# First weight pair of a macaron feed-forward: seven Strassen products for gate and up alike, with two products of the next pair's gate taken ahead

## The chip, the cores and the metric

The kernel runs on one core of a Trainium2 chip. Time is device time in microseconds (us) for one execution. The engines are TensorE (PE, with its weight load PEld), VectorE (DVE), ScalarE (ACT), GpSimd (POOL) and SyncE (SP), which issues nearly all DMAs.

## The reference

One layer: half a SwiGLU feed-forward, two attention mixers side by side, a projection, and a second half feed-forward, each behind an RMS norm, for 1024 tokens of width 1024 in float32. The change touches the first part of the two feed-forwards (D_FF = 2816):

```python
def rms_norm(x, g):
    xf = x.astype(jnp.float32)
    y = xf * lax.rsqrt(jnp.mean(xf * xf, axis=-1, keepdims=True) + EPS)
    return (y * g.astype(jnp.float32)).astype(x.dtype)

def swiglu(h, w_gate, w_up, w_down):
    return (jax.nn.silu(h @ w_gate) * (h @ w_up)) @ w_down

x = x + 0.5 * swiglu(rms_norm(x, g_ffn1[l]), w1_gate[l], w1_up[l], w1_down[l])
...
x = x + 0.5 * swiglu(rms_norm(x, g_ffn2[l]), w2_gate[l], w2_up[l], w2_down[l])
```

## The kernel before, in words

**Numbers as two halves.** TensorE is fed float32 numbers as a rounded high half and a low half that holds the rest. An operand tile has the high half in its columns 0 to 511 (`HI`) and the low half in 512 to 1023 (`LO`). ScalarE writes the high half and GpSimd or VectorE subtracts it to get the low one (`halve`, L379). A product of two operands is then high x high, high x low and low x high over four blocks of 128: 12 matmuls (`times`, L526).

**Strassen's scheme (Winograd's form).** `ffn_in` (L501) makes gate and up, turned so that features lie on partitions. It takes weights in pairs of 128 features: a pair's left matrix has the blocks A11, A12 (first 128 features, first and second half of the width) and A21, A22 (the second 128). The right matrix is the normed input, turned: B11, B21 for the first 512 tokens, B12, B22 for the second 512. With S1 = A21 + A22, S2 = S1 - A11, S3 = A11 - A21, S4 = A12 - S2 and T1 = B12 - B11, T2 = B22 - T1, T3 = B22 - B12, T4 = B21 - T2, the table `FACTORS` (L375) names seven products instead of eight. Product 1 is A11 B11, 2 is A12 B21, 3 is S4 B22, 4 is A22 T4, 5 is S1 T1, 6 is S2 T2 and 7 is S3 T3. B12 itself is in none of them. C11 is 1 + 2 in one PSUM bank; the others are sums of u2 = 1 + 6 with the rest, in which 4 adds into the bank of 7 and 3 into the bank of 5.

**The pairs.** There are 11 pairs in each feed-forward. Pairs 2 to 11 go through `products` (L538), in the order 1, 6, 7, 5, 2, 4, 3, once for gate and once for up. The first pair goes through `opening` (L562), because the second token half comes late: in the first feed-forward its rows are still being loaded and normed, in the second they come out of the projection before it.

**The opening before.** Gate is computed by eight plain half products (`half`, L574) with B11, B21, B12 and B22, up by seven. Six products need the first token half alone: gate's four and up's 1 and 2. Then both turns of the second half (`R.turn`, L435: 16 transposes each) follow, and then nine products. The opening stands under `tc.manual_schedule`: each engine takes its operations in the order of the program text. Outside it a scheduler places the operations, and it can put those of the second pair between the opening's, as their operands allow.

**Around it.** `R.stat` (L420) sums the squares of a token tile on ScalarE, with a small step on VectorE and a power on GpSimd; `R.norm` (L426) scales the tile on VectorE. In the first feed-forward this runs for tiles 4 to 7 within the opening, in the second for tile 7 (the list `rows`). `R.keep` copies turned blocks out of PSUM for the sums T1 to T4, and `R.low` (L483) makes operands of those sums. PSUM has eight banks, two for each letter "a" to "d" (`bank`, L331). `finish` (L675) makes the seven left operands of the down projection for a pair and stores them. `beside` (L879) hangs other work of the kernel onto the pairs' products by count, from the second pair on. The loads of weight tiles (512 KB each) have four places; the second pair's loads reuse those of the first as soon as its blocks are halved.

Of the kernel before, what the change touches and what calls it, by code (L numbers as in the profile page):

```python
# [58 lines left out]
def f32(ap):  # L59
    return ap.bitcast(F32)  # L60
# [187 lines left out]
def trunk(ctx, tc, x, positions, g_ffn1, w1_gate, w1_up, w1_down, g_mix, w_in, g_cq, w_uq_a, w_q_idx,  # L248
# [136 lines left out]
    class Right:  # L385
# [87 lines left out]

        def kept(self):
# [17 lines left out]
    def loader(raw, nm):  # L492
        def load(w, f, name):
            t = raw(name)
# [6 lines left out]
    def ffn_in(nm, R, wg, wu, raw, op, sums, ct, bank, staged, rows, first=None, beside=lambda n, ins: None):  # L501
# [5 lines left out]
        def left_sides(rs, name, pinned, early=False):  # L507
            A11, A12, A21, A22 = (r[:, q] for r in rs for q in (HI, LO))
            O = {n: op(f"{name}{n}") for n in ("A11", "S2", "S3", "S1", "A12", "A22", "S4")}
            s1, s2, s3, s4 = (sums(f"{name}s{n}") for n in range(1, 5))  # L510
            in_turn_ = tc.keep_in_program_order if pinned else lambda i: i
            if early:
                halve(O["A11"], A11)

            def rest():
# [4 lines left out]
                for n, src in (("A11", A11), ("S2", s2), ("S3", s3), ("S1", s1), ("A12", A12), ("A22", A22), ("S4", s4))[early:]:  # L520
                    halve(O[n], src)
                return O

            return rest if early else rest()
# [13 lines left out]
        def products(O, name, nxt):  # L538
            pa = bank("pa", "a")
            mul(O, 1, pa)  # L540
            u2 = ct(f"{name}u2")
            nc.scalar.activation(u2, pa, AF.Copy)
# [11 lines left out]
            mul(O, 2, pa, False)  # L554
# [5 lines left out]
            return (pa, u2, c21, u3), nxt  # L560

        def opening(raws, rows, nxt):  # L562


            A = [dict(zip(("A11", "A12", "A21", "A22"), (r[:, q] for r in rs for q in (HI, LO)))) for rs in raws]
            O = ({}, {})

            def left(e, *names):
                for n in names:
                    O[e][n] = halve(op(f"{nm}{e}0{n}"), A[e][n])  # L570

            ps, sg = {}, {}

            def half(r, c, q, letter=None):  # L574

                if not q:
                    ps[r, c] = bank("pg", letter)
                times(O[0][f"A{r + 1}{q + 1}"], B[f"B{q + 1}{c + 1}"], ps[r, c], not q)

            def gate(r, c):  # L580
                sg[r, c] = ct(f"{nm}sg")
                nc.scalar.activation(sg[r, c], ps[r, c], AF.Silu)

            def up(n, ps_, start=True):
                a, b = FACTORS[n]
                times(O[1][a], B[b], ps_, start)
# [1818 lines left out]
```

## Time and profile before

| | |
|---|---|
| median of 3 runs | 2128.14 us (2124.06 to 2130.36) |
| the profiled execution | 2127.6 us |
| its span, first to last instruction | 2125.8 us |
| mean granted clock of TensorE | 0.998 |
| TensorE, VectorE, ScalarE, GpSimd busy | 99%, 71%, 50%, 43% of the span |
| products of the first opening | 15.2 to 63.4 us |
| products of the second opening | 1485.4 to 1533.5 us |

In a row of a timeline stand the start and the duration in us, the engine, the line of the kernel, the operation, the tile written and the tiles read, the shape, and how many were merged. In brackets is the idle time of the engine before it and what ended that. A name such as `a01A` is tile A of the first feed-forward (a), gate (0), second pair (1). A row of windows gives for each stretch the busy time of PE, PEld, DVE, ACT and POOL, then the granted clock as a share of full speed, the share of the DMA engines and the GB/s.

### The profile page before, as it was taken

Reading aid. Unit: us, or ns where it says so; the run is one execution under the profiler, and the core shown is the slowest. Engines: PE = TensorE matmul, PEld = TensorE weight load, DVE = VectorE, ACT = ScalarE, POOL = GpSimd, SP = SyncE. Lnnn points to the kernel's source line nnn. Section 1 sums busy time; section 2 is a strip of 40 time slices with the busy share of each in tenths; the row PEclk is TensorE's granted clock in tenths of the full one; section 3 lists DMA queues with packets and bytes.
Section 4 is the critical chain, followed back from the end, with each engine's and each line's share of the span. In section 5 each row is a group of like instructions: output and inputs, shape, how many; then the busy total and the mean of one; then the engine's idle time right before and its main releaser. Section 6 shows DMA issues by size and latency. Waiting matters only on the chain.

```text
span 2125.8 us, 29838 instructions
## 1 busy us (share of the span) xinstructions
PE 2105.6 (99%) x10196; PEld 1766.6 (83%) x10196; DVE 1519.8 (71%) x2485; ACT 1056.7 (50%) x1990; POOL 910.6 (43%) x718
## 2 busy tenths in 40 slices
PE   9999999999999999999999999999999999999999
PEld 7888888888889989888878888888888888888887
DVE  7866767678875599788886768844755556487675
ACT  6343343334455356888887667435432322324443
POOL 6654555522346234422113333354664545542233
PEclk9999999999999999999999999999999999999999
DMA  5577877497685252676747744774143333359655
GB/s 150 160 247 216 254 201 239 152 335 248 206 230 167 79 160 92 223 219 178 181 133 232 253 140 134 253 277 139 50 129 99 104 94 126 97 188 327 221 175 188
DMA packets 298104, 387.79 MB, mean 182 GB/s; under 512 B 40144, under 2 KB 186224, under 8 KB 297952
## 3 DMA queue, kind: packets, MB, share of 16 engines
q1 hardware_dynamic: 285088, 343.90, 52.1%
q0 software_dynamic: 12864, 41.99, 5.5%
q8 instruction: 80, 1.31, 0.3%
q14 instruction: 72, 0.59, 0.1%
HBM read 264.67 MB, written 121.15 MB: 181 GB/s over the span
## 4 chain that ended last, share of the span: by engine, by line
PE 90%; DVE 3%; DMA 3%; issue 2%; ACT 1%; POOL 0%; SPq 0%; DVEq 0%; ACTq 0%; POOLq 0%
PE p L769 6%; PE p L770 6%; PE p L768 6%; PE psf L312 4%; PE psf L313 4%; PE psf L314 4%; PE pd L530 4%; PE pd L531 3%; PE pd L529 3%; PE pa L530 3%; PE pc L529 3%; PE pa L531 3%; PE pa L529 3%; PE pc L530 3%; PE pc L531 3%
## 5 line engine op out<-in xcount | busy, mean ns | idle before, releaser
L1369 ACT ACTIVATE junka<-u,cand,sig 128x896 bf16<-128x896 f32 (+3 forms) x124 | 134.6, 1085 | 5.9 <-DVE cand L1361 4.6
L1816 DVE TENSOR_TENSOR_SCAN left<-left,hidden 128x640 f32<-128x640 f32 (+3 forms) x64 | 89.1, 1414 | 2.7 <-ACT left L1810 2.5
L892 ACT ACTIVATE swh<-swr 128x512 fp32r<-128x512 f32 x48 | 30.2, 630 | 116.9 <-issue 48.2
L893 DVE TENSOR_TENSOR swr<-swr,swh 128x512 f32<-128x512 f32 x48 | 44.8, 932 | 39.4 <-ACT swh L892 36.5
L1871 DVE SCALAR_TENSOR_TENSOR pt<-pstT,pt 128x512 fp32r<-128x512 f32 (+1 forms) x96 | 51.7, 550 | 16.5 <-ACT pt L1868 15.7
L672 ACT ACTIVATE b0u<-b0u 128x512 f32<-128x512 f32 x20 | 12.6, 632 | 99.8 <-DVE b0u L552 84.4
L1868 ACT ACTIVATE pt<-pstT 128x512 fp32r<-128x512 f32 (+1 forms) x96 | 46.6, 495 | 24.1 <-PE pstT L1943 23.0
L1721 ACT ACTIVATE relu<-psdot 128x512 f32<-128x512 f32 (+1 forms) x80 | 39.8, 522 | 27.7 <-DVE u L1728 17.9
L769 PE MATMUL p<-aT,aS 128*128 128x512 f32 x132 | 51.6, 391 | 0.9 <-DVE aT L382 0.9
L769 PE MATMUL p<-bT,bS 128*128 128x512 f32 x132 | 51.4, 390 | 0.0
L1230 POOL DMA_DIRECT2D gd<-evg x32 | 18.1, 566 | 76.9 <-ACT evg L1225 66.4
L770 PE MATMUL p<-aT,aS 128*128 128x512 f32 x132 | 50.8, 390 | 0.0
L770 PE MATMUL p<-bT,bS 128*128 128x512 f32 x132 | 50.8, 390 | 0.0
L1728 DVE SCALAR_TENSOR_TENSOR u<-relu,WI,u 128x512 f32<-128x512 f32 (+1 forms) x70 | 46.0, 680 | 2.8 <-ACT relu L1721 1.8
L1943 PE MATMUL pstT<-ident,left 128*128 128x128 f32 x288 | 46.0, 273 | 1.2 <-DVE pt L1871 1.2
L768 PE MATMUL p<-bT,bS 128*128 128x512 f32 x132 | 47.0, 389 | 0.0
L1997 ACT ACTIVATE e<-e,mx 128x1024 f32<-128x1024 f32 (+7 forms) x52 | 40.2, 774 | 10.2 <-DVE mx L1988 9.3
L768 PE MATMUL p<-aT,aS 128*128 128x512 f32 x132 | 44.9, 390 | 0.0
L1943 PEld LDWEIGHTS pstT<-ident,left 128*128 128x128 f32 x288 | 35.6, 140 | 10.6 <-DVE pt L1871 2.4
L1810 ACT ACTIVATE left<-psz 128x512 f32<-128x512 f32 (+2 forms) x96 | 42.9, 506 | 1.9 <-PE psz L1836 1.5
L381 ACT ACTIVATE bT<-bt 128x512 fp32r<-128x512 f32 x44 | 26.3, 625 | 33.9 <-PE p L770 29.4
L1365 DVE TENSOR_SCALAR_CACHE_REDUCE junkv<-u,cand 128x512 uint8<-128x512 f32 (+1 forms) x62 | 41.7, 673 | 0.7
(3065 smaller groups left out, 8141.0 us busy)
## 6 DMA issues: line engine op xcount, KB each, us to landing
aw<-in_w_down_dram SPq DMA_DIRECT2D x33, 512.0 KB, 4.8
bw<-in_w_down_dram SPq DMA_DIRECT2D x33, 512.0 KB, 4.8
swr<-in_w_in_dram SPq DMA_DIRECT2D x48, 256.0 KB, 6.3
a0r<-in_w_gate_dram SPq DMA_DIRECT2D x22, 512.0 KB, 7.8
a1r<-in_w_up_dram SPq DMA_DIRECT2D x22, 512.0 KB, 7.4
b0r<-in_w_gate_dram SPq DMA_DIRECT2D x22, 512.0 KB, 4.2
b1r<-in_w_up_dram SPq DMA_DIRECT2D x22, 512.0 KB, 3.9
x<-in_x_dram SPq DMA_DIRECT2D x16, 512.0 KB, 6.1
```

Of the source, the lines that this page charges most:

```text
L312: nc.tensor.matmul(ps, ah, bh, start=first, stop=False)
L313: nc.tensor.matmul(ps, ah, bl, start=False, stop=False)
L314: nc.tensor.matmul(ps, al, bh, start=False, stop=last)
L529: nc.tensor.matmul(ps, a[:, c], b[k][:, HI], start=start and k == 0, stop=False, skip_group_check=True)
L530: nc.tensor.matmul(ps, a[:, c], b[k][:, LO], start=False, stop=False, skip_group_check=True)
L531: ins = nc.tensor.matmul(ps, a[:, l], b[k][:, HI], start=False, stop=k == 3, skip_group_check=True)
L768: nc.tensor.matmul(ps[q][m], S[:, h], T[:, HI], start=p == 0, stop=False)
L769: nc.tensor.matmul(ps[q][m], S[:, h], T[:, LO], start=False, stop=False)
L770: nc.tensor.matmul(ps[q][m], S[:, l], T[:, HI], start=False, stop=p == last)
L1369: nc.scalar.activation(junks[1][:, 0:(i + 1) * P], score[i], AF.Sign, scale=sig[:, b:b + 1], bias=cand.bitcast(F32)[:, b:b + 1], accum_out ...
L1816: nc.vector.tensor_tensor_scan(back, back, ones, 1.0, op0=ALU.mult, op1=ALU.max)
L1943: nc.tensor.transpose(tp[:, q * P:(q + 1) * P], A[n + q][:, j * P:(j + 1) * P], ident)
```

## The change

In the opening gate goes through the seven products as up does. A third left matrix, the second pair's gate, is halved in part (A11 and A12, loaded once more and earlier into a place of its own), and its products 1 and 2 stand in the opening too. So six products still need the first token half alone, of three matrices, but the third matrix's product 2 comes between the two turns. `products` then leaves out 1 and 2 for that gate. B12 is turned, but no longer made into an operand; three of its four places hold the sums for T2 and the third matrix's load. Gate's S1, S2 and S4 and up's S4 are summed on VectorE, S3 of both on GpSimd. The steps that multiply gate by up and `finish` of the first pair move under the manual order, at its end. The tiles of the token rows are allocated ahead, and SyncE issues the third matrix's load between the loads of token tiles 5 and 6.

```diff
         def turn(self, n, letters="abcd", less=None, between=0, also=None):
-            if n not in self.B:
+            if n not in self.B and n != "B12":
                 self.operands(n)
...
-                t = self.B[n][k]
-                self.keep([(t[:, HI], ps)])
-                self.less([t[:, LO]], [ps], [f32(t[:, HI])])
+                if n in self.B:
+                    t = self.B[n][k]
+                    self.keep([(t[:, HI], ps)])
+                    self.less([t[:, LO]], [ps], [f32(t[:, HI])])
...
+        def third(self, load, w):
+            load(w, 2, f"{self.nm}0r1", self.held[2])
+
+        def hold(self):
+            self.held = [f32(self.tt(f"{self.nm}hold{k}")) for k in range(3)] + [self.tt(f"{self.nm}hold3")]
...
-        def products(O, name, nxt):
-            pa = bank("pa", "a")
-            mul(O, 1, pa)
-            u2 = ct(f"{name}u2")
-            nc.scalar.activation(u2, pa, AF.Copy)
+        def products(O, name, nxt, begun=None):
+            if begun:
+                u2, c11 = begun
+            else:
+                c11 = pa = bank("pa", "a")
+                mul(O, 1, pa)
+                u2 = ct(f"{name}u2")
+                nc.scalar.activation(u2, pa, AF.Copy)
...
-            mul(O, 2, pa, False)
+            if not begun:
+                mul(O, 2, pa, False)
...
+            left("A12", 0, 1)
+            r = R.raw
+            r["T2"] = [t[:, c] for t in R.held[0:2] for c in (HI, LO)]
+
+            def step(t):
                 R.keep(copies[1 + 2 * t:3 + 2 * t], nc.vector)
                 if 4 - t <= len(rows):
                     R.stat(rows[t + len(rows) - 4])
+            step(0)
+            by(0, 1, "a", "a")
+            u2[0] = copied(ct(f"{nm}u2"), 0, "a")
+            step(1)
+            by(1, 1, "a", "b")
+            u2[1] = copied(ct(f"{nm}u2"), 1, "a")
+            left("A11", 2)
+            left("A12", 2)
+            step(2)
+            by(0, 2, "a", start=False)
+            out[0, 0] = copied(ct(f"{nm}sg"), 0, "a", AF.Silu)
+            step(3)
+            fsum("S1", nc.vector, 0, 1)
+            fsum("S2", nc.vector, 0)
+            left("S1", 0, 1)
             for t in rows:
                 R.norm(t)
+            by(1, 2, "a", start=False)
+            fsum("S2", nc.vector, 1)
+            fsum("S4", nc.vector, 0)
+            by(2, 1, "a", "c")
+            u2[2] = copied(ct(f"{nm}u2"), 2, "a")
+            left("S4", 0)
+            nc.vector.tensor_mul(out[0, 0], out[0, 0], ps[1, "a"])
+            fsum("S4", nc.vector, 1)
+            left("S4", 1)
+            R.turn("B12", "dabc", (r["T1"], r["T3"]))
+            by(2, 2, "a", start=False)
             R.low("T1", nc.gpsimd)
+            out[2, 0] = copied(ct(f"{nm}sg"), 2, "a", AF.Silu)
+            R.less(r["T2"], R.turn("B22", "dada"), r["T1"])
+            by(0, 5, "d", "b")
+            by(1, 5, "d", "c")
+            left("S2", 0, 1)
+            u3[0] = copied(R.spare(f"{nm}u3"), 0, "d")
             R.low("T2", nc.vector)
+            u3[1] = copied(R.spare(f"{nm}u3"), 1, "d")
+            fsum("S3", nc.gpsimd, 0, 1)
+            left("S3", 0, 1)
+            by(0, 3, "d", start=False)
+            by(1, 3, "d", start=False)
             R.less(r["T3"], r["T2"], r["T3"])
+            R.less(r["T4"], r["T4"], r["T2"])
             R.low("T3", nc.vector)
+            by(0, 6, "b", "b")
+            nc.vector.tensor_add(u2[0], u2[0], ps[0, "b"])
+            left("A22", 0, 1)
+            by(1, 6, "b", "c")
+            R.low("T4", nc.vector)
+            nc.vector.tensor_add(u2[1], u2[1], ps[1, "b"])
+            nxt = nxt({n: O[2][n] for n in ("A11", "A12")})
+            c12 = [ct(f"{nm}c12") for e in range(2)]
+            for e in range(2):
+                nc.vector.tensor_add(c12[e], u2[e], ps[e, "d"])
+            nc.scalar.activation(c12[0], c12[0], AF.Silu)
+            for e in range(2):
+                by(e, 7, "c", "da"[e])
+                nc.vector.tensor_add(u3[e], u3[e], u2[e])
+                nc.vector.tensor_add(u3[e], u3[e], ps[e, "c"])
+                if not e:
+                    nc.scalar.activation(u3[0], u3[0], AF.Silu)
+            nc.vector.tensor_mul(c12[0], c12[0], c12[1])
             nxt = nxt()
+            nc.vector.tensor_mul(u3[0], u3[0], u3[1])
+            for e in range(2):
+                by(e, 4, "c", start=False)
+                nc.vector.tensor_add(u2[e], u2[e], ps[e, "c"])
+                if not e:
+                    nc.scalar.activation(u2[0], u2[0], AF.Silu)
...
-                    H, u, nxt = opening(first, rows, lambda: lefts(1, 0, early=True))
+                    H, S, begun, nxt = opening(first, R.held[2], rows, lambda made: lefts(1, 0, made=made))
+                    finish(0, H, S, True)
+                continue
...
             for t in range(4, NT):
+                if t == 6:
+                    R.third(load, w1_gate)
                 rows(t)
```

Here `by(e, n, p)` is product n of matrix e (0 gate, 1 up, 2 the second pair's gate) into bank p, with a letter where the bank is new; `left(n, ...)` is `halve` of block n; `fsum` forms one of S1 to S4; `copied` is ScalarE's copy out of a bank, with Silu where named.

More of the change, by code (lines that the diff above doesn't have):

```diff
@@ L559, in products @@
             nc.vector.tensor_add(u2, u2, pd)
[L560 to L569, printed above, removed]
-                    O[e][n] = halve(op(f"{nm}{e}0{n}"), A[e][n])
[L572 to L584, printed above, removed]
+            return (c11, u2, c21, u3), nxt
@@ new lines, in opening, with left, fsum, by @@
+        def opening(raws, third, rows, nxt):
+            A = [dict(zip(("A11", "A12", "A21", "A22"), (r[:, q] for r in rs for q in (HI, LO)))) for rs in (*raws, (third,))]
+            O, S, ps, u2, u3, out = ({}, {}, {}), ({}, {}), {}, {}, {}, {}
+            def left(n, *es):
+                for e in es:
+                    O[e][n] = halve(op(f"{nm}{e}0{n}"), A[e][n])
+            def fsum(n, eng, *es):
+                for e in es:
+                    a, b = {"S1": ("A21", "A22"), "S2": ("S1", "A11"), "S3": ("A11", "A21"), "S4": ("A12", "S2")}[n]
+                    A[e][n] = sums(f"{nm}{e}{n}")
+                    (eng.tensor_add if n == "S1" else eng.tensor_sub)(A[e][n], A[e][a], A[e][b])
+            def by(e, n, p, letter=None, start=True):
+                if letter:
+                    ps[e, p] = bank(f"p{p}", letter)
@@ L585, in up, with copied @@
                 a, b = FACTORS[n]
-                times(O[1][a], B[b], ps_, start)
+                times(O[e][a], B[b], ps[e, p], start)
+            def copied(to, e, p, func=AF.Copy):
+                nc.scalar.activation(to, ps[e, p], func)
+                return to
             if "B11" not in B:
-                left(0, "A11")
-                R.operands("B12", "B11", "B21", "B22", "T1")
+                left("A11", 0)
+                R.operands("B11", "B21", "B22", "T1")
                 R.kept()
@@ L596, in opening @@
                 copies += zip(R.raw["T4"], p21)
-                left(0, "A21", "A22")
                 R.second()
@@ L606, in opening @@
                     R.stat(rows[t + len(rows) - 4])
-                left(1, *n)
-            r = R.raw
-            r["T2"] = [R.spare(f"{nm}r22{k}") for k in range(4)]
-            S = {n: sums(f"{nm}s{n}") for n in ("S1", "S2", "S3", "S4")}
-            A11, A12, A21, A22 = (A[1][n] for n in ("A11", "A12", "A21", "A22"))
-            nc.vector.tensor_add(S["S1"], A21, A22)
-            nc.vector.tensor_sub(S["S2"], S["S1"], A11)
-            A[1].update(S)
+            step(0)
+            by(0, 1, "a", "a")
@@ L618, in opening @@
-            half(0, 0, 1)
-            gate(0, 0)
-            left(1, "S2")
-            half(1, 0, 0, "b")
-            pa = bank("pa", "a")
-            up(1, pa)
-            u2 = ct(f"{nm}u2")
-            half(1, 0, 1)
-            nc.scalar.activation(u2, pa, AF.Copy)
-            gate(1, 0)
-            left(1, "S1")
-            up(2, pa, False)
-            R.turn("B12", "cdab", (r["T1"], r["T3"]))
-            nc.gpsimd.tensor_sub(S["S3"], A11, A21)
-            nc.gpsimd.tensor_sub(S["S4"], A12, S["S2"])
@@ L633, in opening @@
-            left(1, "S3")
-            R.less(r["T2"], R.turn("B22", "bcdc"), r["T1"])
-            R.low("T1", nc.gpsimd)
-            half(0, 1, 0, "d")
-            half(1, 1, 0, "b")
-            R.low("T2", nc.vector)
-            left(1, "S4", "A22")
-            half(0, 1, 1)
-            gate(0, 1)
-            half(1, 1, 1)
-            gate(1, 1)
+            by(1, 2, "a", start=False)
+            fsum("S2", nc.vector, 1)
+            fsum("S4", nc.vector, 0)
+            by(2, 1, "a", "c")
@@ L2332, in trunk @@
             x1 = residual(1)
-            R = Right(g_ffn2, bank, fp(op), ct, ct, tt, ts, in_turn((sums, 3), (ct, 1)), "b")
+            R = Right(g_ffn2, bank, fp(op), ct, ct, tt, ts, ct, "b")
             def between():
-                R.operands("B12")
+                R.hold()
                 R.kept()
```

87 lines of the change are left out of this document (36 added, 51 removed).

## The prediction

> **What bounds the kernel now.** I read the first page, then the timelines of the engines over the first feed-forward's opening (0 to 80 us), then over the second's (1480 to 1560).
>
> ```profile
> span 2125.8 us, 29838 instructions
> PE 2105.6 (99%) x10196; PEld 1766.6 (83%) x10196; DVE 1519.8 (71%) x2485; ACT 1056.7 (50%) x1990; POOL 910.6 (43%) x718
> ```
>
> TensorE (PE) is busy for 2105.6 of 2125.8 us. A matmul left out is therefore time saved, as long as the operands of the next one are ready. TensorE's rows (start, duration, idle time before it and what ended that):
>
> ```profile
> 15.20 0.47 PE L529 MATMUL pg<-aB,a00A 128*128 128x512 f32 x1
> 23.47 0.39 PE L529 MATMUL pa<-aB,a10A 128*128 128x512 f32 x1
> 26.19 0.39 PE L529 MATMUL pg<-aB,a00A 128*128 128x512 f32 x1
> 31.64 3.65 PE L443 MATMUL pst<-ident,x 128*128 128x128 f32 x32
> 35.87 0.47 PE L529 MATMUL pg<-aB,a00A 128*128 128x512 f32 x1 [0.57 <-ACT aB L464]
> 53.89 0.39 PE L529 MATMUL pa<-aB,a01A 128*128 128x512 f32 x1
> 57.29 0.39 PE L530 MATMUL pa<-aB,a01A 128*128 128x512 f32 x1
> 60.46 0.46 PE L529 MATMUL pc<-aT,a10A 128*128 128x512 f32 x1
> 75.44 0.51 PE L529 MATMUL pc<-aT,a01A 128*128 128x512 f32 x1 [0.44 <-DVE a0u L549]
> 1501.67 3.65 PE L443 MATMUL pst<-ident,x 128*128 128x128 f32 x32
> 1505.90 0.47 PE L529 MATMUL pg<-bB,b00A 128*128 128x512 f32 x1 [0.57 <-ACT bB L464]
> ```
>
> A product of 12 matmuls takes 2.72 us (23.47 to 26.19, 0.227 each). Six products run from 15.20 to 31.64, then the 32 transposes of the second token half (0.114 each, 1.82 for a turn of 16), then the rest. TensorE waits 0.57 in each opening and 0.44 in the pair after the first. The rows 53.89 and 57.29 are the second pair's product 1, put among the opening's last products. The opening's last product starts at 60.46, right behind the VectorE (DVE) addition that empties its bank:
>
> ```profile
> 59.63 0.67 DVE L659 TENSOR_TENSOR au<-au,pc 128x512 f32<-128x512 f32 x1
> ```
>
> Without those 12 matmuls it would have been due 2.7 us earlier. So VectorE already ends the opening one product late, and the second pair's product 1 is what covers that.
>
> **The change part by part.** *Saved.* Each opening and its next gate go from 22 to 21 products: 2.72 us, twice is 5.44. If the quoted waits go too (0.57 + 0.57 + 0.44 = 1.58) it is 7.0. The eight operations that made B12 an operand go as well, beside TensorE.
>
> *A bank wait, first opening only.* Up's product 1 moves from fourth place to second and takes the older "b" bank. That bank is free after the first of the two copies in the second row:
>
> ```profile
> 14.60 4.68 DVE L470 SCALAR_TENSOR_TENSOR aB<-pst,agcol,aB 128x512 fp32r<-128x512 f32 x7
> 19.20 1.39 DVE L462 TENSOR_SCALAR araw<-pst,agcol 128x512 f32<-128x512 f32 x2
> ```
>
> The copy ends at 19.9, and VectorE runs it behind the seven operations above. TensorE is there at 15.20 + 2.72 = 17.9: **2.0 us**, and the product ends at 22.6.
>
> *The norm of the last token tile.* ScalarE (ACT) keeps the written order. New in it: the last tile's sum of squares stands behind a copy of product (up, 1), two halvings of the third matrix and the first Silu with its table load.
>
> ```profile
> 17.52 1.20 ACT L381 ACTIVATE a00A<-a0r 128x512 fp32r<-128x512 f32 x2
> 18.56 1.10 ACT L423 ACTIVATE aj<-x 128x1024 bf16<-128x1024 f32 x1
> 19.60 0.68 ACT L381 ACTIVATE a10A<-a1r 128x512 fp32r<-128x512 f32 x1
> 23.93 1.28 ACT L582 ACT_TABLE_LOAD   x1
> 25.22 0.60 ACT L582 ACTIVATE asg<-pg 128x512 f32<-128x512 f32 x1
> ```
>
> From start to start a 512-wide operation takes 0.52 and a sum of squares 1.04. So: copy from 22.9, halvings to 24.4, tile 6's sum to 25.5, table to 26.8, Silu to 27.3, tile 7's sum, readable at 28.5. VectorE, held by its small step on that sum, then has three operand sums (0.60 each) and four norms:
>
> ```profile
> L429 DVE TENSOR_SCALAR x<-x,rs x4: 740/748/1777, 25.6 to 28.6; 128x1024 f32<-128x1024 f32 x4
> 43.54 2.48 DVE L490 TENSOR_TENSOR aT<-ar,aT 128x512 fp32r<-128x512 f32 x4
> 38.12 5.05 POOL L490 TENSOR_TENSOR aT<-araw,aT 128x512 fp32r<-128x512 f32 x4 [1.55 <-ACT aT L488]
> ```
>
> 28.5 + 1.8 + 4 x 0.75 = 33.3. TensorE has three more products before B12's turn, 22.6 + 8.2 = 30.8, and 0.3 of transposes that need no tile 7: **2.2 us** (4.2 if GpSimd slows two norms to 1.78). In the second opening that sum also moves behind the Silu, but the norm (1498.2, below) comes before TensorE (1498.95).
>
> *The low halves of T1.* Product 5 now follows B22's turn at once and needs T1, whose low halves GpSimd (POOL) makes behind those of S1 and S4 for two matrices: eight in a row, 1.26 each, 10.1. If VectorE's stream lets it in only after the norms and two sums (34.5), with about 0.5 more between, they end at 45.1. TensorE: B12 turned at 34.8, product (third, 2), B22's turn, and 2.27 until the fourth low half is used: 41.6. A wait of 3.5. Second opening: it begins at 1501.67 - 6 x 2.72 = 1485.35; the third product ends at 1493.5, ScalarE gives the sum by 1495.6, VectorE the norm by 1498.2 and two sums by 1499.4, GpSimd ends at 1510.0, TensorE needs it at 1507.6: 2.4. If GpSimd gets in at 1497 it is 1.3.
>
> *VectorE's list up to product 4.* Gate's product 4 adds into the bank that gate's u3 must first have read. From the end of B22's turn VectorE has 8 operations on B22 and T2 (0.66: 5.3), 20 of 0.60 for the low halves of T2, T3, T4 and the sums T3, T4 (12.0), and six additions (3.6): 20.9. Then 1.0, because T2's high halves stand on ScalarE behind a copy of product (gate, 5). TensorE has 8 products, 21.8. On VectorE's time alone it would nearly fit. But GpSimd now has work in that stretch without a break: S3's sums and low halves and A22's, six operations where there were two.
>
> ```profile
> 44.88 7.10 POOL L382 TENSOR_TENSOR a10S<-asS,a10S 128x512 fp32r<-128x512 f32 x1 [1.71 <-ACT a10S L381]
> 67.40 3.43 POOL L382 TENSOR_TENSOR a01A<-a0r,a01A 128x512 fp32r<-128x512 f32 x2
> 69.61 1.78 DVE L679 TENSOR_TENSOR au<-asg 128x512 f32<-128x512 f32 x1
> 71.31 1.78 DVE L678 TENSOR_TENSOR au<-ac,asg 128x512 f32<-128x512 f32 x1
> ```
>
> Where GpSimd works in a row, the two engines alternate, and VectorE's operations come 1.70 apart instead of 0.60; a GpSimd operation that arrives from idle waits for the whole stream instead (7.10). The first is this case: 6 x 1.10 = 6.6. So 20.9 + 1.0 + 6.6 + 0.2 - 21.8 = **6.9 us** in each opening, the T1 wait included, and 1.0 more (**7.9**) in the first, where product 5 and with it the copy are later. The bounds: without alternation the T1 waits alone remain, 3.5 and 2.4.
>
> The Trainium skill (SBUF — State Buffer, "Who interferes with whom") says that whichever engine issues first has the shared port pair for one whole instruction while the other is blocked. The 1.78 rows agree; the 7.10 does not, since 5.8 us beyond the usual 1.26 are more than nine VectorE operations of 0.60. If VectorE held the pair in that way here too, S3 would come late instead, and the sum changes by about 1 us.
>
> *The second pair.* Its product 1, the cover named above, is spent. Its product 4 writes a bank that VectorE reads behind the five operations that end the first pair, three or four of them at 1.78 beside five GpSimd halvings: TensorE comes 13.6 after product (gate, 4) starts, VectorE is through at about 14.8: **1.2** each. The 0.44 was this wait in small.
>
> *Moved at no cost.* The third matrix's load stands on SyncE (SP) ahead of the last two token tiles. One 512 KB load is worth 1.35:
>
> ```profile
> 7.85 1.06 ACT L423 ACTIVATE ay<-x 128x1024 bf16<-128x1024 f32 x1 [1.00 <-DMA x<-in_x_dram]
> 9.20 1.06 ACT L423 ACTIVATE ay<-x 128x1024 bf16<-128x1024 f32 x1 [0.20 <-DMA x<-in_x_dram]
> ```
>
> The last tile's sum of squares moves back by about 4, so the later landing is covered; uncovered it would be 1.35. The second pair's reloads start later, when A22 is halved, with some 4 us to spare.
>
> **Sum.** The profiled execution took 2127.6 (span 2125.8 and 1.8 around it; the median of the runs, 2128.14, is 0.5 above). First opening 2.0 + 2.2 + 7.9 + 1.2 = 13.3, second 6.9 + 1.2 = 8.1, less 7.0: +14.4, **2142.0 us**.
>
> **Rivals.** *Everything fits* (the other side): GpSimd and VectorE keep up, all waits vanish, 2127.6 - 7.0 = 2120.6. Against it: the bank wait follows from rows that stay as they are. Chance 0.04.
>
> *No alternation:* VectorE's list stays near 22. The alternation decides from its third operation on: 20.9 + 1.0 + 0.2 + 3 x 1.10 - 21.8 = 3.6 is just over the T1 wait. Then 2.0 + 2.2 + 3.5 + 2.4 - 7.0 = +3.1, 2130.7, no measurable change. For it: the 7.10 row. Against it: GpSimd starts from idle there. Chance 0.16.
>
> *The clock falls in the waits.* The only dip inside the span:
>
> ```profile
> 1218.07 0.45 PE L2035 MATMUL psL<-kkh,qs 128*128 128x384 f32 x1 [1.81 <-DVE mx L1988]
> 1215.00:1222.00 7.00, 4.63 (x16) 3.15 (x17) 6.87 (x23) 5.22 (x18) 3.75 (x3) 0.75 1.09 359
> 1222.00:1230.00 8.00, 8.00 (x41) 7.14 (x40) 3.80 (x8) 5.10 (x11) 0.00 (x0) 0.79 0.37 120
> ```
>
> A stretch with waits around 1.81 us was followed by granted clocks of 0.75 and 0.79 over 7 and 8 us, that is 6.9 us at half speed, 3.4 lost. A wait of 3 to 4 us before product 4 could do the same. The slower TensorE would absorb the 1.2 behind it: 2.2 net per dip, 2146.4 for two, 2150.8 for four. Chance 0.32. The Trainium skill (TensorE: Matmul & The Clock Gate, Part 1) asks for an idle window of about 3.4 us; by that not every such wait would trip it, while the row shows a dip after less.
>
> **How the numbers follow.** The forecast has 0.48 and goes from 2136 (fewer alternations) to 2146. The range runs from the no-alternation case to four dips, 2130 to 2151. About 6.4 us (0.3%) is what a measurement can tell: faster 0.04, same 0.16, slower 0.80.
>
> **What would show it.** The profile of after should show waits of TensorE ended by VectorE: about 2 at the second product, 2 at B12's turn, short ones on GpSimd's T1 in product 5, and 3 to 5 before gate's product 4 in both openings; VectorE operations at 1.78 between B22's turn and T3. Wrong would be a T2-to-T4 stream at 0.60 throughout, or product 4 without a wait.

## The result, and the profile after

The changed kernel takes 2155.8 us (median of 4 runs, 2154.6 to 2158.7) against 2128.5 for the kernel before: ratio 1.0131, 95% interval 1.0116 to 1.0146. It is slower, as forecast, but by 27 us and not by 14, outside the range. The profiled execution took 2154.56, its span 2152.4.

Where the time went is read from the same eight matmuls in both traces, four in each feed-forward: the first product of the opening, the second pair's up product 6 (the first product behind the last one that the prediction priced), and the first and last matmul of the down projection. First the timeline of the kernel before (start, duration, engine, line, operation and tiles; its first product, at 15.20, stands in the prediction), then of the kernel after:

```profile
83.09 0.39 PE L529 MATMUL pb<-aT,a11S 128*128 128x512 f32 x1
442.13 0.39 PE L768 MATMUL p<-aT,aS 128*128 128x512 f32 x1
656.22 0.39 PE L770 MATMUL p<-aB,aA 128*128 128x512 f32 x1
1485.35 0.39 PE L529 MATMUL pg<-bB,b00A 128*128 128x512 f32 x1
1553.10 0.39 PE L529 MATMUL pb<-bT,b11S 128*128 128x512 f32 x1
1912.14 0.39 PE L768 MATMUL p<-bT,bS 128*128 128x512 f32 x1
2121.35 0.39 PE L770 MATMUL p<-bB,bA 128*128 128x512 f32 x1
```

```profile
span 2152.4 us, 29797 instructions
15.06 0.47 PE L538 MATMUL pa<-aB,a00A 128*128 128x512 f32 x1
93.58 0.39 PE L538 MATMUL pb<-aT,a11S 128*128 128x512 f32 x1
455.74 0.39 PE L804 MATMUL p<-aT,aS 128*128 128x512 f32 x1
673.64 0.39 PE L806 MATMUL p<-aB,aA 128*128 128x512 f32 x1
1504.30 0.39 PE L538 MATMUL pa<-bB,b00A 128*128 128x512 f32 x1
1577.92 0.39 PE L538 MATMUL pb<-bT,b11S 128*128 128x512 f32 x1
1936.96 0.39 PE L804 MATMUL p<-bT,bS 128*128 128x512 f32 x1
2148.09 0.39 PE L806 MATMUL p<-bB,bA 128*128 128x512 f32 x1
```

The differences of neighbouring rows are the lengths of the stages. The last four columns are the same differences in the traces of four experiments told below.

| stage, us | before | after | more | op_phase | outside_restored | before_shifted | s3_left_out |
|---|---|---|---|---|---|---|---|
| first opening, to the second pair's up product 6 | 67.89 | 78.52 | 10.63 | 76.54 | 76.76 | 67.84 | 71.17 |
| rest of the pairs, first feed-forward | 359.04 | 362.16 | 3.12 | 361.95 | 359.04 | 359.04 | 359.85 |
| first down projection | 214.09 | 217.90 | 3.81 | 215.01 | 216.83 | 218.61 | 217.21 |
| between the feed-forwards | 829.13 | 830.66 | 1.53 | 833.72 | 828.51 | 829.03 | 828.12 |
| second opening | 67.75 | 73.62 | 5.87 | 73.58 | 72.69 | 67.71 | 66.66 |
| rest of the pairs, second feed-forward | 359.04 | 359.04 | 0.00 | 359.04 | 359.04 | 359.04 | 359.04 |
| second down projection | 209.21 | 211.13 | 1.92 | 209.21 | 209.21 | 210.06 | 209.21 |

The two openings cost 16.5 us; the prediction had 14.4. The other 10.4 us lie in stages whose code the change does not touch. One caution on the first opening: its first product starts between 15.0 and 17.2 us among the traces, and the wait ahead of up's product 1 is the shorter the later that is (1.90 us in the kernel after, 0.36 in op_phase, which starts at 17.20). First openings compare to within about 1.5 us only. TensorE's waits in the kernel after (what waited, what ended it: us in all, times, longest):

```profile
PE pc L538 <- DVE bu L682: 4.2, 1, 4.2
PE pc L538 <- DVE au L682: 4.2, 1, 4.2
PE pst L443 <- DVE x L429: 3.0, 4, 1.3
PE pa L538 <- ACT a0u L554: 2.8, 1, 2.8
PE pa L538 <- DVE araw L463: 1.9, 1, 1.9
PE pd L539 <- POOL bT L499: 1.6, 4, 0.7
```

Five of the six are places that the prediction named: product 4 in each opening, B12's turn, up's product 1 and T1 in the second opening. The fourth row is not: it is in the third pair. And the granted clock fell in the openings (windows of the kernel after; the share behind POOL's busy time is TensorE's clock):

```profile
32.00:41.00 9.00, 6.95 (x25) 5.65 (x26) 8.29 (x12) 3.79 (x6) 5.18 (x4) 0.62 0.08 30
70.00:75.00 5.00, 4.91 (x15) 3.90 (x16) 4.80 (x8) 2.22 (x4) 0.93 (x1) 0.66 0.00 0
1552.00:1559.00 7.00, 5.50 (x13) 4.42 (x14) 6.76 (x10) 2.92 (x7) 1.57 (x2) 0.51 0.03 6
```

9 x 0.38 + 5 x 0.34 + 7 x 0.49 = 8.5 us of TensorE's time, part of it in windows where it also waited.

### The profile page after: what moved, and what is told of

It reads as the page before. It is cut to its first block, busy times and chain, and to the rows that moved or that the text cites. A ratio compares the mean times of both kernels' runs of the same rounds, so it can differ in the third digit from the quotient of the medians.

```text
span 2152.4 us, 29797 instructions
## 1 busy us (share of the span) xinstructions
PE 2108.7 (98%) x10172; PEld 1764.5 (82%) x10172; DVE 1535.8 (71%) x2495; ACT 1061.2 (49%) x1994; POOL 911.6 (42%) x724
## 4 chain that ended last, share of the span: by engine, by line
PE 85%; DVE 8%; DMA 3%; issue 2%; ACT 1%; POOL 1%; SPq 0%; DVEq 0%; ACTq 0%; POOLq 0%
PE p L805 6%; PE p L806 6%; PE p L804 6%; PE psf L312 4%; PE psf L313 4%; PE psf L314 4%; PE pc L538 4%; PE pc L540 4%; PE pc L539 4%; PE pa L538 3%; PE pd L540 3%; PE pd L539 3%; PE pd L538 3%; PE pa L540 3%; PE pa L539 3%
## 5 line engine op out<-in xcount | busy, mean ns | idle before, releaser
L927 DVE TENSOR_TENSOR swr<-swr,swh 128x512 f32<-128x512 f32 x48 | 49.9, 1040 | 23.2 <-ACT swh L926 21.5
L1908 DVE SCALAR_TENSOR_TENSOR pt<-pstT,pt 128x512 fp32r<-128x512 f32 (+1 forms) x96 | 51.7, 550 | 16.5 <-ACT pt L1905 15.5
```

## The experiments

Two questions. Where do the 10 us outside the openings come from? And what makes VectorE late in the openings: GpSimd beside it, the order of its queue, or the amount of its work?

### Outside the openings: the phase of a ring

Operands take their places in turn from nine, four in one pool and five in another (`ring`). Through the second pair's gate the kernel before takes 18 places (4 + 7 + 7), the changed one 21 (7 + 7 + 2 + 5). All later operands thus fall three places further on. Likewise the ring of results gives 12 places up to the third pair where it gave 14, and `beside` counts two products fewer.

**op_phase.**

```diff
-    def in_turn(*sources):
+    def in_turn(*sources, first=0):
...
-        at = [0]
+        at = [first]
...
-        op = in_turn((wt, 4), (lambda name: pool.tile([P, 1024], F32R, tag="r", name=name, bufs=NR), NR))
+        op = in_turn((wt, 4), (lambda name: pool.tile([P, 1024], F32R, tag="r", name=name, bufs=NR), NR), first=6)
```

> The changed kernel, whose ring of nine operand slots (four and five, taken in turn) starts six places later, so that after both openings, which take 21 slots where the kernel before took 18, the next operand falls on the same place of the ring as before. Nothing else is altered. Theory 1, ring phase: of the 27.3 us lost, those that arise in the two down projections and between the two feed-forward blocks (3.4, 1.9 and about 1.5) come from this shift alone: 2149 us, 5 to 7 below the changed kernel, with the openings' waits as they are (1.9, 3.0, 4.2, 4.2). Rival, lateness: these losses follow from what the openings leave behind (transfers and work that start later); then 2155.8, no change.

2147.3 us, ratio 1.0095 (1.0080 to 1.0110): 0.36%, some 8 us, less than the changed kernel. The table shows where 4.8 of them lie: 2.9 in the first down projection and all of the 1.9 in the second. The rest of the 8 no stage of the trace shows. The stage between the feed-forwards shows nothing of the kind; it scatters over 826 to 834 among the traces, more than the 1.5 in question, so that piece stays unexplained.

**before_shifted**, the mirror of it: the kernel before, with the same edit and `first=3`.

> The kernel before, without any part of the change, whose ring of operand slots starts three places later: the phase that the changed kernel has after its openings. Its openings issue what they issued. Theory 1, ring phase: it loses in the down projections what the changed kernel loses there, 5 to 7 us: 2134 to 2135 us. Rival, lateness: 2128.5 us, no change, since nothing in its openings is late.

2136.3 us, ratio 1.0034 (1.0021 to 1.0047), 7 us slower with nothing of the change in it. Its trace loses 4.5 in the first down projection and 0.9 in the second. The same waits stand there in both kernels, TensorE's timeline and GpSimd's operation behind the first of them, first in the kernel after:

```profile
593.74 0.50 PE L806 MATMUL p<-aT,aS 128*128 128x512 f32 x1 [0.57 <-POOL aS L382]
602.97 0.50 PE L805 MATMUL p<-aB,aS 128*128 128x512 f32 x1 [1.41 <-DVE aB L382]
608.42 0.50 PE L805 MATMUL p<-aT,aS 128*128 128x512 f32 x1 [1.74 <-DVE aT L382]
586.28 7.41 POOL L382 TENSOR_TENSOR aS<-aS33r,aS 128x512 fp32r<-128x512 f32 x1 [7.51 <-ACT aS L381]
```

then in before_shifted:

```profile
581.37 0.50 PE L770 MATMUL p<-aT,aS 128*128 128x512 f32 x1 [0.57 <-POOL aS L382]
590.24 0.50 PE L769 MATMUL p<-aB,aS 128*128 128x512 f32 x1 [1.08 <-DVE aB L382]
595.55 0.50 PE L769 MATMUL p<-aT,aS 128*128 128x512 f32 x1 [1.61 <-DVE aT L382]
573.91 7.41 POOL L382 TENSOR_TENSOR aS<-aS33r,aS 128x512 fp32r<-128x512 f32 x1 [7.51 <-ACT aS L381]
```

The same operand, the same 7.41 us for an operation that takes 1.26 elsewhere, the same three waits in a row: the phase alone makes them. So the lateness rival falls for these waits. TensorE's products there stand in another order in these two kernels than in the kernel before and in op_phase. The way from the phase to that order is argued, not shown: which of the two pools an operand falls into changes when its place comes free, and the scheduler places the products and halvings by that. The lateness rival keeps a remainder: op_phase has one wait of 1.84 there, the kernel before one of 0.91, with TensorE's products in the same order.

**before_shifted_six**, the same with `first=6`:

> The kernel before with its ring of operand slots started six places later, where before_shifted started it three places later and lost 0.3%. If any other phase changes the order of the down projections for the worse, 2132 to 2137 us; if some phases are as good as the one that the kernel had, 2127 to 2130.

2129.3 us, ratio 1.0003 (0.9994 to 1.0012); down projections of 213.95 and 209.21, with the products in another order again. So a shifted phase is not bad in itself. The one that the change happened to give is.

**outside_restored.** On top of op_phase, the result ring skips two places ahead of the third pair, and `beside` begins at its third entry:

```diff
...
+            if p == 2 and hasattr(ct, "at"):
+                ct.at[0] += 2
...
                 at, turn[0] = turn[0], turn[0] + 1
+                if not at:
+                    agenda[2] = agenda.pop(0) + agenda.pop(1) + agenda[2]
+                    at, turn[0] = 2, 3
```

> The run op_phase and two more edits outside the openings: the result ring's turn is advanced by two places ahead of the third pair (the second pair's gate takes two slots fewer than before), and the list of w_in's loads, splits and stores starts two products in, so that each stands beside the product that it stood beside before. Everything outside the two openings and the second pair's gate is then ordered as in the kernel before. Theory 1: only the openings' own cost is left, 16.4 us over the two: 2128.5 + 16.4 + about 0.5 = 2145.5 us, the 2.8 us wait in the third pair is gone, and the lag of same-named products behind the kernel before stays level from the second pair to the second opening. Rival, lateness: 2153 to 2156, with the lag still growing in the down projections.

2147.6 us, ratio 1.0089 (1.0074 to 1.0104); the profiled execution 2145.1. In the trace the rest of the first feed-forward's pairs is back at 359.04. The 2.8 us in the third pair had been ScalarE's copy of product 1, waiting for a place that a store still held (ScalarE's timeline of the kernel after):

```profile
125.83 0.60 ACT L554 ACTIVATE a0u<-pa 128x512 f32<-128x512 f32 x1 [6.93 <-DMA staged<-a1u]
```

The two edits were not tried apart; that the skipped places are what cured it follows from this row, not from a run. In the times the 3 us do not show against op_phase (the intervals overlap); in the trace they do. The first down projection, at 216.8, is 2.7 longer than before, with products and halvings in the order of the kernel before. The trace shows what this is made of: the one wait there is 1.85 us in place of 0.91, and the clock fell behind it, which it does not do in the kernel before (windows, first of the kernel before, then of outside_restored; the clock is the third number from the end):

```profile
600.00:640.00 40.00, 39.09 (x177) 32.10 (x176) 27.93 (x36) 21.86 (x39) 18.94 (x16) 1.00 0.85 236
600.00:640.00 40.00, 38.15 (x161) 31.07 (x161) 27.22 (x37) 20.52 (x37) 14.00 (x9) 0.96 0.86 215
```

The 0.9 of the wait and 40 x 0.04 = 1.6 of the clock are nearly all of the 2.7. Behind the wait stands a load of an operand that was staged in memory (aS310r). It is issued 159.4 to 159.6 us after the stage's first matmul in the kernel before, in op_phase and in outside_restored alike, but from issue to landing it took 11.2 us in the first and 12.3 in the other two. So for this wait it is the transfer and not a later issue; why the transfer took longer is open.

### In the openings: what makes VectorE late

All further kernels start from outside_restored, where only the openings differ from the kernel before.

**s3_left_out.** S3 is not formed and not split; product 7 uses S2's operand, so part of gate and up is another quantity. Two of ScalarE's halvings go with it, and the ring starts at 8 instead of 6, so that its phase behind the openings stays the same.

```diff
-            fsum("S3", nc.gpsimd, 0, 1)
-            left("S3", 0, 1)
+            for e in range(2):
+                O[e]["S3"] = O[e]["S2"]
```

> outside_restored with one sum left out in both openings: S3 of the first pair's gate and up is neither formed nor split on GpSimd, and product 7 takes S2's operand in its place, so that part of the result differs; the ring starts so that its phase after the openings is the same. TensorE has the same products. Theory 2, contention: the four T2 low halves on VectorE took 6.47 us because they alternated with these four GpSimd operations; without them they take 2.5 us, the 4.2 us wait ahead of the gate's product 4 shrinks to under 0.5 in each opening, the half clock that followed it (70.7 and 1552) is gone, and the time is 8 to 12 us below outside_restored. Rival, VectorE's queue is late for another reason (the 2.9 us that it stands idle at 40.3 to 43.2 waiting for ScalarE's copies, and its longer list of sums): the wait shrinks by 1 us or less.

2133.4 us, ratio 1.0017 (1.0006 to 1.0028): some 15 us less than outside_restored. The openings fall by 5.6 and 6.0 us in the traces. VectorE's T2 low halves and the wait ahead of the gate's product 4, first in outside_restored:

```profile
48.51 6.79 DVE L500 TENSOR_TENSOR aT<-ahold,aT 128x512 fp32r<-128x512 f32 x4
70.47 0.77 PE L539 MATMUL pc<-aT,a00A 128*128 128x512 f32 x1 [4.14 <-DVE au L683]
```

then in s3_left_out:

```profile
48.57 2.49 DVE L500 TENSOR_TENSOR aT<-ahold,aT 128x512 fp32r<-128x512 f32 x4
66.22 0.47 PE L539 MATMUL pc<-aT,a00A 128*128 128x512 f32 x1 [0.45 <-DVE au L683]
```

The four operations start at the same time and take 2.49 in place of 6.79: four GpSimd operations beside them had cost VectorE 1.08 each. This is the prediction's alternation price (1.10), taken away and measured. The wait is 3.7 us shorter in the first opening and 4.0 in the second (4.15 against 0.18); most of the rest is the clock, which no longer falls behind the wait (15 x 0.11 = 1.7 us; the window of outside_restored, then of s3_left_out):

```profile
60.00:75.00 15.00, 10.61 (x40) 8.02 (x39) 14.70 (x23) 6.25 (x12) 4.50 (x3) 0.89 0.25 70
60.00:75.00 15.00, 14.55 (x65) 11.74 (x64) 14.72 (x20) 5.22 (x9) 5.94 (x4) 1.00 0.41 123
```

**vector_doubled**, the other way round:

```diff
             R.low("T3", nc.vector)
+            R.less([t[:, LO] for t in B["T3"]], r["T3"], [f32(t[:, HI]) for t in B["T3"]])
```

> outside_restored, and in both openings VectorE forms T3's four low halves twice (the second time with the same result): 4 x 0.60 = 2.4 us more on VectorE per opening and nothing on any other engine. If VectorE's total bounds the openings, the wait ahead of the gate's product 4 grows from 4.2 to 6.6 us and the time by 4.8 us, to 2152. If something else holds product 4 back, or VectorE has slack behind it, the growth is under 1.5 us.

2151.0 us, ratio 1.0104 (1.0090 to 1.0119), 3.4 us more in the medians. The openings are 79.52 and 75.05 us long, 2.8 and 2.4 more than in outside_restored, for 2.4 us of VectorE's work; of the 2.8, 0.9 is the longer wait at up's product 1 (1.77 against 0.87), which this edit does not touch. So by the traces most of VectorE's added work is on the path. The wait is now in two places:

```profile
63.93 0.50 PE L540 MATMUL pc<-aT,a00S 128*128 128x512 f32 x1 [2.56 <-DVE aT L474]
73.59 0.47 PE L539 MATMUL pc<-aT,a00A 128*128 128x512 f32 x1 [2.53 <-DVE au L684]
```

**own_bank.** Product 4 no longer waits for the reading of product 7; VectorE's additions and the next sums change places:

```diff
...
-                by(e, 4, "c", start=False)
-                nc.vector.tensor_add(u2[e], u2[e], ps[e, "c"])
+                by(e, 4, "f", "da"[e])
+                nc.vector.tensor_add(u2[e], u2[e], ps[e, "f"])
```

> outside_restored; in both openings the gate's and up's product 4 goes into a bank of its own instead of being added onto product 7's, so that it no longer waits until VectorE has read product 7; VectorE adds product 7 and product 4 to u2 one after the other (two more additions), does the additions of product 6 behind T4's low halves, and forms the second pair's four sums ahead of the first pair's last combinations. Theory 3, the order of VectorE's queue is what delays product 4: the 4.2 us wait falls to under 1 us in both openings, the half clock behind it goes, and the time is 7 to 12 us below outside_restored (2136 to 2140). Rival, VectorE is full whatever stands first: the wait moves on to the second pair's product 6, which needs the second pair's sums split, and the time is less than 3 us below.

2145.1 us, ratio 1.0071 (1.0057 to 1.0085). The 4.2 us wait is gone, and the next one is there, in the second pair's product 4:

```profile
87.14 0.79 PE L539 MATMUL pc<-aT,a01A 128*128 128x512 f32 x1 [3.06 <-DVE a0u L562]
```

The rival had the right kind of outcome but named product 6; its bound of 3 us holds in the medians (2.4, with intervals that overlap). The profiled execution, at 2145.9, is no faster than that of outside_restored: the second opening is 1.9 shorter and the first 3.7 longer, with a wait of 1.91 at up's product 1 and granted clocks of 0.89 from 15 to 30 us and 0.66 from 85 to 95.

**front_reordered.** One of B11's banks is read earlier, and the sums of squares and norms stand ahead of the Silu and of S1's and S2's sums:

```diff
+                R.keep(copies[1:2], nc.vector)
                 left("A11", 1)
                 p21 = R.turn("B21")
...
             left("A11", 2)
-            left("A12", 2)
             step(2)
+            step(3)
+            left("A12", 2)
             by(0, 2, "a", start=False)
             out[0, 0] = copied(ct(f"{nm}sg"), 0, "a", AF.Silu)
-            step(3)
+            for t in rows:
+                R.norm(t)
...
```

> outside_restored; in the first opening VectorE reads one bank of B11's turn ahead of B21's low halves, so that up's product 1 finds its bank free, and ScalarE squares the last two token tiles ahead of product 2's Silu with its table load, VectorE norms the tiles ahead of the sums S1 and S2. Theory: the wait of 1.9 us ahead of up's product 1 and the 3.0 us of norms ahead of B12's turn are gone, with them the half clock of 6.8 us that began at 33.2 (3.4 us): 5 to 8 us below outside_restored, 2140 to 2142. Rival, VectorE's total bounds the first opening: the 5 us reappear ahead of the gate's product 4, whose wait grows from 4.2 to about 8, and the time falls by 2 us or less. The second opening, where three of the four tiles are normed beforehand, should show no change.

2145.9 us, ratio 1.0076 (1.0060 to 1.0093), which does not tell it from outside_restored. The waits at up's product 1 (1.9 in the kernel after, 0.87 in outside_restored) and of the norms (3.0) are gone from the trace; the first opening is 1.1 us shorter. Part of what it gained is waited for later, at B22's turn and T1 (0.71 and 1.40 us), and part goes in the clock, which fell to 0.77 in the window from 60 to 75 (0.89 in outside_restored). Ahead of product 4 nothing became better:

```profile
68.24 0.76 PE L539 MATMUL pc<-aT,a00A 128*128 128x512 f32 x1 [4.16 <-DVE au L684]
```

The rival's "about 8" did not come either: TensorE and VectorE both reached that place sooner, by about as much.

**s3_on_vector.** S3's sums stand on VectorE, behind S4's, and the halves directly behind S2's:

```diff
-                    A[e][n] = sums(f"{nm}{e}{n}")
+                    A[e][n] = A[e]["A21"] if n == "S3" else sums(f"{nm}{e}{n}")
...
+            fsum("S3", nc.vector, 0, 1)
...
+            left("S3", 0, 1)
...
-            fsum("S3", nc.gpsimd, 0, 1)
-            left("S3", 0, 1)
```

> outside_restored; in both openings S3's two sums are formed on VectorE, in place over A21, beside the other sums, and their low halves follow S2's on GpSimd directly, so that two of the four GpSimd operations no longer fall beside VectorE's T2 low halves. Theory 2, contention by the operation: each GpSimd operation beside a run of VectorE two-input operations costs VectorE about 1 us, so the T2 low halves take about 4.5 us in place of 6.47, and the time is 3 to 5 us below outside_restored (2142 to 2144). Rival: the sums' own 1.2 us on VectorE eats the gain, 2146 to 2148.

2143.5 us, ratio 1.0065 (1.0050 to 1.0079), about 4 us down in the medians, though the intervals touch; in the traces the openings are 0.8 and 0.9 shorter. T2's low halves take 4.80 us (two operations beside them in place of four), product 4's wait is 2.41.

**all_three.** The three together.

> The edits of own_bank, front_reordered and s3_on_vector together. If the three waits are separate, their gains add up and the openings come near their saved product: 16.4 us less 15 to 20, 2126 to 2131 us, about the kernel before, perhaps 2 us faster. Rival, one engine's total (VectorE with GpSimd beside it) bounds the openings: the gains overlap, and the time stays above 2135.

2141.3 us, ratio 1.0062 (1.0047 to 1.0076). The gains did not add up. The wait had moved again, ahead of B22's turn, whose bank VectorE read late:

```profile
39.98 1.97 PE L444 MATMUL pst<-ident,x 128*128 128x128 f32 x8 [4.15 <-DVE araw L472]
```

**b12_first.** In all_three's kernel VectorE takes B12's readings ahead of the sums S2, S4 and S3:

```diff
-            fsum("S2", nc.vector, 0)
             left("S1", 0, 1)
...
-            fsum("S2", nc.vector, 1)
-            fsum("S4", nc.vector, 0)
...
-            fsum("S4", nc.vector, 1)
-            fsum("S3", nc.vector, 0, 1)
-            left("S4", 1)
             R.turn("B12", "dabc", (r["T1"], r["T3"]))
+            fsum("S2", nc.vector, 0, 1)
...
             R.less(r["T2"], R.turn("B22", "dada"), r["T1"])
+            fsum("S4", nc.vector, 0, 1)
+            left("S4", 0, 1)
+            fsum("S3", nc.vector, 0, 1)
```

> all_three with VectorE's queue put in another order in both openings: the four readings of B12's turn stand directly behind the norms and S1's sums, ahead of S2's, S4's and S3's sums and of the product of gate and up, which now stand behind B22's readings. In all_three VectorE formed those sums first at 1.76 us each beside GpSimd and TensorE waited 4.15 us for a bank at B22's turn. If VectorE with GpSimd beside it bounds the opening through its order, that wait goes, T1's low halves come about 6 us sooner, and the time falls by 4 to 8 us against all_three: 2133 to 2137 us. If only the total counts, whatever the order, the time stays within 2 us of all_three's 2141.

2146.7 us, ratio 1.0082 (1.0068 to 1.0096), 5 us slower than all_three in the medians, and 4.7 in the openings of the traces. The wait at B22's turn was gone, but ScalarE's copy of product 5 now stood behind S3's halvings, and product 3 waited for it:

```profile
47.85 0.80 PE L539 MATMUL pd<-aB,a00S 128*128 128x512 f32 x1 [4.82 <-ACT au L599]
```

Neither expectation fits: the order of ScalarE's queue had been left out of both.

**norms_on_scalar.** Two of b12_first's norms on ScalarE (`nc.scalar.activation(xt, xt, AF.Copy, scale=self.rs[t])`), ahead of product 2's Silu.

> b12_first, and in the first opening two of the four norms of the second token half (0.93 us each on VectorE) go to ScalarE, which is idle at that place for some microseconds. If VectorE's total is the bound, the first opening ends 1.5 to 2 us sooner and the time falls by as much; if the order or another engine is the bound, it does not change. The second opening is as in b12_first.

2149.3 us, ratio 1.0085 (1.0071 to 1.0100): no change that can be told. The first opening is 0.4 shorter. The wait for ScalarE's copy (4.71 here, 4.82 above) still stood ahead of product 3, so the run says little of VectorE's total.

**order_mended.** From b12_first: S4's sums too stand behind B12's readings, S3's sums and halves behind T2's low halves.

```diff
             R.turn("B12", "dabc", (r["T1"], r["T3"]))
             fsum("S2", nc.vector, 0, 1)
+            fsum("S4", nc.vector, 0, 1)
...
-            fsum("S4", nc.vector, 0, 1)
             left("S4", 0, 1)
...
-            fsum("S3", nc.vector, 0, 1)
...
-            left("S3", 0, 1)
             u3[0] = copied(R.spare(f"{nm}u3"), 0, "d")
             R.low("T2", nc.vector)
             u3[1] = copied(R.spare(f"{nm}u3"), 1, "d")
+            fsum("S3", nc.vector, 0, 1)
+            left("S3", 0, 1)
```

> b12_first, in which ScalarE copied the up's product 5 out of its bank behind the halves of S3 and TensorE stood for 4.8 us ahead of product 3: now S2's and S4's sums stand behind B12's readings, S3's sums behind T2's low halves, and ScalarE makes that copy and T2's high halves ahead of S3's. If the order of the queues was what b12_first lost by, the 4.8 us wait goes and the time falls to 2136 to 2140 us, below all_three's 2141. If VectorE's total bounds the openings, the time stays at 2141 to 2146: the same work in another order.

2139.3 us, ratio 1.0048 (1.0036 to 1.0060), the lowest median of these kernels that computes everything, and still 10 us behind the kernel before. Its openings are 71.88 and 70.21 us, 4.0 and 2.5 over the kernel before (the second to product 5, which stands first there); 1.2 more lie in the pairs behind the first opening and 2.6 in the first down projection. Of VectorE's queue:

```profile
33.81 1.74 DVE L590 TENSOR_TENSOR a0S<-a0S,a0r 128x512 f32<-128x512 f32 x1
46.41 2.48 DVE L500 TENSOR_TENSOR aT<-ahold,aT 128x512 fp32r<-128x512 f32 x4
57.25 6.82 DVE L500 TENSOR_TENSOR aT<-ar,aT 128x512 fp32r<-128x512 f32 x4
```

T2's low halves are free of GpSimd now (2.48), but the sums ahead of them are not (1.74 each) and T4's low halves have taken the burden over (6.82 where the kernel after had 4.09). The largest wait that is left in either opening is not for VectorE but for GpSimd: one low half of S3, which comes from idle while VectorE works without a break, takes 8.16 us (and again 8.16 in the second opening), and product 7 waits for it:

```profile
50.29 8.16 POOL L383 TENSOR_TENSOR a00S<-a0r,a00S 128x512 fp32r<-128x512 f32 x1 [4.76 <-PE pd L541]
58.51 0.50 PE L541 MATMUL pc<-aT,a00S 128*128 128x512 f32 x1 [2.44 <-POOL a00S L383]
```

This is the form that the prediction set aside, with S3 late instead of VectorE. So the order matters by some microseconds, and moving work about mostly moves the contention. None of these kernels beats the kernel before.

## Why the prediction was wrong

**Right.** The direction, and most of the mechanism: the opening is one product late on VectorE, the cover is spent, GpSimd alternates with VectorE at 1.70, and TensorE waits ahead of product 4 in both openings. T2's low halves took 6.47 and T4's 4.09 in place of 2.48 each, 5.6 us of alternation against the 6.6 of the prediction. Up's product 1 waited 1.90 (predicted 2.0). The norms held up B12's turn by 3.0 (2.2): the four took 4.77 us, not 4 x 0.75, so the wait lies between the term and its bound of 4.2.

**Mis-sized.** Product 4 with the T1 wait was put at 7.9 and 6.9. The first opening showed 4.2 and no T1 wait worth the name, the second 4.2 + 1.6 = 5.8. In the first, GpSimd ended T1's low halves at 45.04, as predicted (45.1), but TensorE came to product 5 only at 43.43, where the prediction's terms give 34.8 + 2.72 + 1.82 = 39.3: 0.8 of that from the norms and 3.4 from the slow clock from 33 to 40 us. That this hid the T1 wait is argued from the rows; in own_bank, at full clock there, a wait of 0.8 appears. The 1.2 in the second pair did not appear at all; own_bank, where a wait of 3.06 stands there, suggests that it was only covered by the wait ahead. In all, the openings' waits came to 9.2 and 5.8 us, 15.0 where the sum had 21.4. The clock dips, a rival with a chance of 0.32, did come, three of them, and took up to 8.5 us that the sum had at nothing. Smaller waits and added dips nearly cancel, and that the openings' 16.5 us come so near to 14.4 is luck in that part.

**The step that failed** is the sum: "First opening 13.3, second 8.1, less 7.0". It stopped at the second pair, as if an opening could be later or sooner but could not change what follows. "Moved at no cost" counted loads. It did not count what the change takes from shared rings: three operand places more, two result places fewer, two counts of `beside`. What the runs showed in place of that nothing is 10.4 us behind the openings. 4.8 of them, in the two down projections, go when op_phase restores the operands' phase, and before_shifted puts 5.4 into the down projections of a kernel that is otherwise unchanged; in the times the phase is worth some 8 and 7 us, of which the traces place no more than this. 3.1 lie in the pairs behind the first opening, where the result ring's row shows 2.8 us for a place that a store still held. 0.9 stays in the first down projection in op_phase, behind a load that took longer, and 1.5 lies between the feed-forwards, within that stage's scatter. The rest of the miss is the 2.1 us in the openings (16.5 less 14.4).

**The saving was real and lost on another engine.** s3_left_out has the same products as the changed kernel, and with four GpSimd operations fewer its second opening is 1.1 us shorter than the kernel before (66.66 against 67.75); its first is still 3.3 longer. A product less on TensorE brought nothing, because the change pays for it with operand sums and halvings on VectorE and GpSimd, in the one stretch where VectorE was already late.

## What to carry to other kernels

Before counting what a saved product is worth, look at which engine ends the stretch: here VectorE and GpSimd made the operands in time by one product only, each GpSimd operation beside VectorE's low halves cost VectorE 1.1 us, and most of VectorE's added work showed in the opening's length. An edit that allocates a different number of tiles from a ring shifts the places of everything behind it, which cost 7 us at one phase and nothing at another; count the places, restore the phase first, and only then judge the edit. And a wait removed from a queue that is full comes back at the next place that needs the queue: add up the engine's work in the stretch, with its neighbours, before moving single waits.

## What the runs showed of the hardware

GpSimd does not disturb every kind of VectorE operation. In the kernel after, T1's four low halves on GpSimd took 1.26 each, and VectorE, which read PSUM beside the last two of them, took 0.66 for each operation, as when it is alone. Its next four such operations, from 45.82, took as long beside GpSimd operations of 1.29 and 1.30. The alternation came with VectorE's operations on two SBUF tiles, and two of the four norms took 1.77:

```profile
40.01 5.03 POOL L499 TENSOR_TENSOR aT<-araw,aT 128x512 fp32r<-128x512 f32 x4
43.17 2.73 DVE L471 SCALAR_TENSOR_TENSOR aB<-pst,agcol,aB 128x512 fp32r<-128x512 f32 x4 [2.89 <-ACT aB L465]
```

The Trainium skill (GPSIMD Engine Reference, Specifications) names VectorE instructions with two SBUF inputs, or in a 2-port mode, as those that contend with GpSimd; these rows agree. Whether the norms ran in such a mode no row shows. The prediction's price held per operation. The other form, a GpSimd operation from idle that waits for VectorE's whole stream, came as well (7.41 after 7.51 us of idle time, and 8.16 after 4.76 in order_mended).

The clock fell to half (0.50 granted from 22 to 24 us in own_bank) after waits that were short one by one. Ahead of the dip at 33 us TensorE had waited 1.32 and 1.28 us, with one transpose between:

```profile
32.40 0.30 PE L443 MATMUL pst<-ident,x 128*128 128x128 f32 x1 [1.32 <-DVE x L429]
33.98 0.48 PE L443 MATMUL pst<-ident,x 128*128 128x128 f32 x1 [1.28 <-DVE x L429]
```

After the wait of 1.90 us at 19.95 the clock stayed at 1.00 in the kernel after; in own_bank the same wait (1.91, at 20.16) was followed by a fall, as the window from 15 to 30 us shows:

```profile
15.00:30.00 15.00, 13.09 (x53) 10.39 (x52) 9.24 (x17) 11.66 (x20) 7.96 (x8) 0.89 0.65 183
```

And the waits of 1.15 and 1.28 us ahead of own_bank's norms, at 34.10 and 35.68, were not followed by a fall: its clock was 1.00 from 30 to 45 us, where the kernel after had fallen. So nearly the same waits went either way in two executions. How long or how dense the waits must be was not tried.
